# Four rotary-table instructions moved within the value stage, and the doubled keys of mixer B made by GpSimd: a two-layer encoder on one core

## The chip, the cores and the metric

The kernel runs on one core of a Trainium2 chip. Its engines are TensorE (PE in the profile; its weight loads are PEld), VectorE (DVE), ScalarE (ACT), GpSimd (POOL) and SyncE (SP), each with a queue of its own that it works off in order; they wait for each other through semaphores. The metric is the device time of one execution in microseconds (us). Three executions of the kernel before took 1438.0, 1436.29 and 1437.93 us, the median is 1437.93 us.

## The reference

The input is one sequence of 512 positions with 1024 channels, float32. Two layers follow each other; each is a token mixer and a squared-ReLU MLP, with a residual around each:

```python
def reference(x, ...):
    for i in range(DEPTH):                       # DEPTH = 2
        h = rms_norm(x, norm_mix[i])
        if i % 2 == 0: y = dilated_mixer(h, ...) # mixer A
        else:          y = mla_mixer(h, ...)     # mixer B
        x = x + y
        h = rms_norm(x, norm_ffn[i])
        a = jax.nn.relu(h @ w1); x = x + (a * a) @ w2
```

Mixer A projects to queries, keys and values for three groups of eight heads of 128 channels. Queries and keys are normalised per head, scaled by a gain and rotated:

```python
qkv = (h @ w_qkv).reshape(B, S, 3, N_GROUPS, A_HEADS, A_HEAD_DIM)
for g, (window, dil) in enumerate(DIL_CONFIGS):
    q = rope(rms_norm(qkv[:, :, 0, g], q_gain[g]), S)
    k = rope(rms_norm(qkv[:, :, 1, g], k_gain[g]), S)
    o, lse = dilated_group(q, k, qkv[:, :, 2, g], window, dil)
```

`rope(x)` is `x * cos + rot * sin`, where `rot` is x with its halves exchanged and one of them negated. Mixer B is latent attention with eight heads. A key there has 128 channels of its own head and 64 rotated channels that all heads share; the norm runs over all 192:

```python
k = jnp.concatenate([k_nope, broadcast(k_rope)], -1)
k = rms_norm(k, k_gain)
k = jnp.concatenate([k[..., :128], rope(k[..., 128:], S)], -1)
```

## The kernel before, in words

The program is one function, written with a tile framework. Which instruction stands where in an engine's queue is set by the framework's scheduler, by its own forecast of costs, and not only by the order of the code: an edit at one place can move instructions at others. `tc.issue_after(mark)` makes it put what stands under it behind the marked instruction. Pools hand out tiles in turn; a transfer into a tile waits for the last reader of what was there.

All matrix products run in float32 split in two: a weight `b` becomes `whi` (a ScalarE copy, L406 or L157) and `wlo` (VectorE's `b - whi`, L407 or L158), and each product is three matmuls, high by high, high by low, low by high.

**The value stage** (`v_phase`, some 9 to 130 us) makes mixer A's values for six heads of each of the three groups g = 0, 1, 2. Tokens, input channels and output columns are each cut in two, and seven products of blocks replace eight. Group 0 runs first, woven with the norm and the transposition of the input (`norm`, `turn`, `Ssp`, `hT`); `piece(g, ba)` makes products 5, 3, 6, 7 and 4 of a group. Four weight blocks `b11`, `b21`, `b12`, `b22` come by DMA for each group (L328, SP's queue); `add_block` (L334, VectorE, two instructions of 128x768) makes their sums `bT` and `b3`. A product accumulates into two PSUM tiles, and `put` (L433 to L443) brings them to `vo`: a ScalarE copy (L438) for the first, a VectorE add or subtract of 128x384 (L440) for the others. A product that takes the same PSUM tile must wait for that `put`.

After `piece(0, ba)` a tile `rot` gets cosines, sines and gains by three DMAs on SP (L515 and L305), and `tables(0, ...)` (L256 to L265, called at L518) makes group 0's tables from it: four VectorE multiplies of 128x512, `cosg` (L260) and `sing` (L263), two each. Their first reader is the evacuation of queries and keys (`qk_evac`), in the stage after the values. Then the loop over g = 1, 2 does the same seven products with loads one group ahead.

**Mixer B** (some 885 to 1075 us) goes by pairs of heads. For each pair and each 128 positions, `kv_chunk` projects keys and values (matmuls at L1028), sums squares on ScalarE into `junkb` (L137), gets the reciprocal root `krs` (VectorE L129, then a power on GpSimd, L132), and makes `ks`, the scaled keys (VectorE, L1082), and `kd`: the shared rotated key `krr` times the head's `krs`, written twice side by side (ScalarE, L1085, two instructions of 128x128 with `krs` as scale). TensorE transposes `ks` and `kd` (L124), and ScalarE and VectorE bring them out as `kn` (L1095) and `kr` (L1098). `q_chunk` does the like for queries: `r` (VectorE, L1049), `rd` (GpSimd, L1053, 128x256), `qn`, `qr`. `score` and `pv_b` are the attention of the pair (L1110, L1134). There are 16 key chunks in all, four for each of four pairs.

Of the kernel before, what the change touches and what calls it, by code (L numbers as in the profile page):

```python
# [12 lines left out]
AF = mybir.ActivationFunctionType  # L13
ALU = mybir.AluOpType
# [3 lines left out]
P = 128  # L18
# [8 lines left out]
QL, KVL, RD = 256, 128, 64  # L27
# [60 lines left out]
def encoder_kernel(ctx: ExitStack, tc: tile.TileContext, x, norm_mix, norm_ffn, a_w_qkv, a_q_gain, a_k_gain,  # L88
# [3 lines left out]
    V, A, G, PE = nc.vector, nc.scalar, nc.gpsimd, nc.tensor  # L92
    uid = [0]
    marks = {}

    def nm(s):
        uid[0] += 1
        return f"{s}_{uid[0]}"
# [24 lines left out]
    def transpose(o, i):  # L123
        PE.transpose(o, i, ident)  # L124
# [10 lines left out]
    def mean_square(junk, x, dim, out):  # L135

        A.activation(junk, x, AF.Square, scale=1.0 / math.sqrt(dim), accum_out=out)  # L137
# [118 lines left out]
    def tables(g, gqk, cos, sin):  # L256

        for t in range(2):
            gb = gqk[:, t].rearrange("p (f d) -> p f d", f=2).unsqueeze(1).broadcast_to([P, NT, 2, 64])
            V.tensor_tensor(cosg[g][:, :, t].rearrange("p r (f d) -> p r f d", f=2),  # L260
                            cos.rearrange("p (r d) -> p r d", r=NT).unsqueeze(2).broadcast_to([P, NT, 2, 64]), gb,
                            op=ALU.mult)
            V.tensor_tensor(sing[g][:, :, t].rearrange("p r (f d) -> p r f d", f=2),  # L263
                            sin.rearrange("p (r f d) -> p r f d", r=NT, f=2), gb, op=ALU.mult)
# [38 lines left out]
    def load_gains(g, gqk):  # L303
        for t, src in enumerate((a_q_gain, a_k_gain)):
            nc.sync.dma_start(gqk[:, t], src[0, g].partition_broadcast(P))  # L305

    def v_phase(vp):
# [17 lines left out]
        def block(g, ki, ni, name):  # L325
            t = vp.tile([P, 4, VH], F32, tag="wq", name=nm(name), bufs=6)
            for u in range(2):
                nc.sync.dma_start(t[:, 2 * u:2 * u + 2], wblk(g, ki, ni, u))  # L328
            return t

        def add_block(t, x, y):
            for u in range(2):
                us = slice(2 * u, 2 * u + 2)
                V.tensor_tensor(t[:, us], x[:, us], y[:, us], op=ALU.add)  # L334
# [89 lines left out]
        def both(p, w, banks, first):  # L424
            for u, t in ((0, 0), (0, 1), (1, 0), (1, 1)):
                product(p, w, banks, first, u, t)

        def new_banks(chain):
            pl, tg = {"a": (sc_p, "sc"), "b": (tp_p, "tp"), "d": (acc_p, "acc")}[chain]
            return [pl.tile([P, 512], F32, tag=tg, name=nm(tg)) for _ in range(2)]  # L430

        def put(g, i, n, how, banks, last):

            o = vo[:, 2 * i + n]
            for t in range(2):
                acc = banks[t][:, :VH]
                if how == "set":
                    A.activation(o[:, t], acc, AF.Copy)  # L438
                else:
                    V.tensor_tensor(o[:, t], o[:, t], acc, op=ALU.add if how == "add" else ALU.subtract)  # L440
                if last:

                    nc.gpsimd.dma_start(vall[g].rearrange("(m r) d -> m r d", r=NT)  # L443
                                        [:, 2 * i + t, VH * n:VH * n + VH], o[:, t])
# [19 lines left out]
        def sum_tile():  # L464
            return vp.tile([P, 4, VH], F32, tag="wq", name=nm("bT"), bufs=6)
# [48 lines left out]
        rot = vp.tile([P, D], F32, tag="xn", name="rot", bufs=2)  # L514
        nc.sync.dma_start(rot[:, 0:C_M1 - C_KEEP], consts[:, C_KEEP:C_M1])  # L515
        g0 = rot[:, 768:1024].rearrange("p (t d) -> p t d", t=2)
        load_gains(0, g0)
        tables(0, g0, rot[:, 0:256], rot[:, 256:768])  # L518
        for g in range(1, NG):
            b21[g] = block(g, 1, 0, "b21")  # L520
            b11[g] = block(g, 0, 0, "b11")
            b12[g] = block(g, 0, 1, "b12")
            b22[g] = block(g, 1, 1, "b22")
            bT[g] = sum_tile()
            parts = {}
            bd, ba = new_banks("d"), new_banks("a")
            both(2, b21[g], bd, True)
            put(g, 0, 0, "set", bd, False)
            both(1, b11[g], ba, True)
            put(g, 0, 0, "add", ba, True)  # L530
            add_block(bT[g], b11[g], b12[g])
            piece(g, ba)

# [3 lines left out]
    with tc.tile_pool(name="vph", bufs=1, reuse_waits="tile") as vp:  # L537
        v_phase(vp)
# [408 lines left out]
    if True:  # L947
        with tc.tile_pool(name="bpool", bufs=1, reuse_waits="tile") as bp, \
# [22 lines left out]
            krr = bp.tile([P, NT, RD], F32, name="krr")  # L971
# [100 lines left out]
            def kv_chunk(d, r):  # L1072
                acc = proj(d, "wkv", r, 2, 512)
                a4 = acc.rearrange("p (h c d) -> p h c d", h=2, c=2)
                junk = bw.tile([P, QL], F32, tag="junkb", name=nm("junkb"), bufs=1)
                ss = st.tile([P, 8], F32, tag="kss", name=nm("kss"))
                for h in range(2):
                    mean_square(junk[:, 0:DH], a4[:, h, 0], QKD, ss[:, h:h + 1])
                rs = rstd_of(ss[:, 0:2], 2, ssr[:, r:r + 1], "krs")
                A.activation(d["v"][:, r], a4[:, :, 1], AF.Copy)  # L1080
                ks = bw.tile([P, 2, DH], F32, tag="ks", name=nm("ks"), bufs=2)
                V.tensor_tensor(ks, a4[:, :, 0], rs.unsqueeze(2).broadcast_to([P, 2, DH]), op=ALU.mult)  # L1082
                kd = bw.tile([P, 2, 2, RD], F32, tag="kd", name=nm("kd"), bufs=2)
                for h in range(2):
                    A.activation(kd[:, h], krr[:, r].unsqueeze(1).broadcast_to([P, 2, RD]), AF.Copy, scale=rs[:, h:h + 1])  # L1085

                def part2():
                    tp = tp_p.tile([P, 512], F32, tag="tp", name=nm("tp"))
                    for h in range(2):
                        transpose(tp[:, h * P:(h + 1) * P], ks[:, h])  # L1090
                        transpose(tp[:, (2 + h) * P:(3 + h) * P], kd[:, h].rearrange("p c d -> p (c d)"))
                    tv = tp.rearrange("p (c t) -> p c t", c=4)
                    sl = slice(r * P, (r + 1) * P)
                    kn, kr = d["kn"], d["kr"]
                    A.activation(kn[:, :, 0, sl], tv[:, 0:2], AF.Copy, scale=gn[:, 1:2])  # L1095
                    V.scalar_tensor_tensor(kn[:, :, 1, sl], tv[:, 0:2], gn[:, 1:2], kn[:, :, 0, sl].bitcast(F32),
                                           op0=ALU.mult, op1=ALU.subtract)
                    A.activation(kr[:, :, 0, sl], tv[:, 2:4], AF.Copy)  # L1098
                    V.tensor_tensor(kr[:, :, 1, sl], tv[:, 2:4], kr[:, :, 0, sl].bitcast(F32), op=ALU.subtract)
                return part2  # L1100
# [122 lines left out]
```

## Time and profile before

| what | value |
|---|---|
| median of three runs | 1437.93 us |
| the profiled execution, its span | 1438.19 us, 1436.4 us |
| mean clock granted to TensorE | 0.996 |
| PE, DVE, ACT, POOL busy | 1400.1, 938.3, 748.6, 208.4 us |
| chain of work that ended last | PE 88%, DVE 5%, ACT 3%, DMA 2% |

The span runs from the first instruction to the last; the rest of an execution's time lies around it. "PE sc L421 <- DVE vo L440: 4.6, 3, 3.1" reads: TensorE's matmuls of line 421 into tile `sc` waited for the VectorE instruction of line 440 that writes `vo`, 4.6 us in total, three times, at most 3.1 us. In a timeline a row has its start, its duration, engine, line, operation, tiles and shape; "x6" joins six alike, and brackets hold the idle time ahead of it and what ended that. Instructions of VectorE and matmuls overlap at their ends, so the distance from one start to the next is what one costs.

### The profile page before, as it was taken

To read this page: it belongs to the slowest core of one execution; us is meant where nothing else is said; L and a number is where in the kernel's file an instruction comes from. 1 tells how busy PE (TensorE), PEld (TensorE's weight loads), DVE (VectorE), ACT (ScalarE), POOL (GpSimd) and SP (SyncE) were. 2 spreads that over 40 slices of the span, in tenths; PEclk is the share of its full clock that TensorE was granted. 3 is DMA by queue.
4 is the path that set the end of the run, shared out by engine and by line. 5 is a ranking of instruction groups with operands and counts; after the bars stand their busy time and mean duration, and the time that the engine had idled before them with its cause. 6 is when DMAs were issued, how large, how long until landed. Compare 5 with 4: busy or idle time off the path is not lost.

```text
span 1436.4 us, 19249 instructions
## 1 busy us (share of the span) xinstructions
PE 1400.1 (97%) x7044; PEld 1186.7 (83%) x7044; DVE 938.3 (65%) x1497; ACT 748.6 (52%) x1626; POOL 208.4 (15%) x224
## 2 busy tenths in 40 slices
PE   7899999999999999999999999999999999999998
PEld 7899888888888988888888887766768888888886
DVE  6876778676876754465564759688755266475647
ACT  6453656464564623553545455777633453544543
POOL 1111212121112001020110203322201010020201
PEclk9999999999999999999999999999999999999999
DMA  9434322332312345667493854210114759394835
GB/s 321 155 132 143 107 88 66 112 98 79 118 60 78 119 135 183 183 130 222 114 235 101 205 121 92 72 31 30 32 44 161 190 114 238 90 231 134 190 89 117
DMA packets 121086, 185.25 MB, mean 129 GB/s; under 512 B 8416, under 2 KB 58336, under 8 KB 120992
## 3 DMA queue, kind: packets, MB, share of 16 engines
q1 hardware_dynamic: 101808, 144.96, 31.5%
q0 software_dynamic: 19184, 39.07, 15.1%
q8 instruction: 55, 0.90, 0.2%
q14 instruction: 39, 0.32, 0.1%
HBM read 176.13 MB, written 7.86 MB: 128 GB/s over the span
## 4 chain that ended last, share of the span: by engine, by line
PE 88%; DVE 5%; ACT 3%; DMA 2%; issue 1%; SPq 0%; POOL 0%; DVEq 0%; ACTq 0%
PE acc L185 51%; PE sc L848 11%; PE tp L848 7%; PE tp L124 4%; PE sc L421 3%; PE tp L421 2%; PE acc L1134 2%; PE sc L1028 1%; PE acc L1110 1%; DVE wlo L792 1%; PE sco L697 1%; PE sc L583 1%; PE sco L693 1%; DMA b<-in_a_w_qkv_dram 1%; PE sc L1110 1%
## 5 line engine op out<-in xcount | busy, mean ns | idle before, releaser
L185 PE MATMUL acc<-whi,hT 128*128 128x512 f32 (+2 forms) x1216 | 384.3, 390 | 2.6 <-ACT hT L735 1.3
L185 PE MATMUL acc<-hT_f,whi 128*128 128x512 f32 (+1 forms) x1152 | 320.2, 368 | 1.7 <-DVE resid L911 1.2
L158 DVE TENSOR_TENSOR wlo<-raw,whi 128x1024 fp32r<-128x1024 f32 (+3 forms) x146 | 172.1, 1187 | 178.4 <-ACT whi L157 178.1
L185 PEld LDWEIGHTS acc<-whi,hT 128*128 128x128 f32 x1216 | 225.3, 188 | 42.7 <-ACT hT L735 1.9
L185 PEld LDWEIGHTS acc<-hT_f,whi 128*128 128x128 f32 x1152 | 209.3, 190 | 37.3 <-DVE resid L911 1.6
L185 PE MATMUL acc<-wlo,hT 128*128 128x512 f32 (+2 forms) x608 | 235.9, 389 | 0.0
L157 ACT ACTIVATE whi<-raw 128x1024 fp32r<-128x1024 f32 (+3 forms) x146 | 149.8, 1031 | 162.0 <-PE acc L185 67.9
L792 DVE TENSOR_TENSOR wlo<-wqs,whi 128x1024 fp32r<-128x1024 f32 x112 | 137.8, 1231 | 112.6 <-ACT whi L791 112.5
L185 PE MATMUL acc<-hT_f,wlo 128*128 128x512 f32 (+1 forms) x576 | 205.6, 367 | 0.0
L791 ACT ACTIVATE whi<-wqs 128x1024 fp32r<-128x1024 f32 x112 | 118.8, 1061 | 159.8 <-PE acc L185 65.8
L848 PE MATMUL sc<-whi,asp 128*128 128x512 f32 x512 | 165.0, 390 | 0.8 <-DVE resid L822 0.7
L777 POOL DMA_DIRECT2D wqs<-in_ffn_w_dram x64 | 77.6, 1344 | 547.9 <-DVE wlo L792 365.0
L185 PEld LDWEIGHTS acc<-wlo,hT 128*128 128x128 f32 x608 | 114.4, 188 | 18.7 <-issue 0.2
L185 PEld LDWEIGHTS acc<-hT_f,wlo 128*128 128x128 f32 x576 | 109.2, 190 | 17.6
L848 PE MATMUL tp<-whi,asp 128*128 128x512 f32 x352 | 112.2, 390 | 1.8 <-DVE resid L822 1.8
L848 PEld LDWEIGHTS sc<-whi,asp 128*128 128x128 f32 x512 | 96.1, 188 | 21.5 <-issue 1.6
L132 POOL TENSOR_TENSOR qrs<-rs_v,nhalf 128x4 f32<-128x4 f32 x48 | 58.7, 1228 | 288.8 <-DVE rs_v L129 239.7
L848 PE MATMUL sc<-wlo,asp 128*128 128x512 f32 x256 | 99.6, 389 | 0.0
L137 ACT ACTIVATE junk<-acc 128x128 f32<-128x128 f32 x192 | 53.1, 277 | 55.7 <-PE acc L185 50.6
L848 PEld LDWEIGHTS tp<-whi,asp 128*128 128x128 f32 x352 | 66.1, 188 | 16.4 <-DVE resid L822 2.7
L848 PE MATMUL tp<-wlo,asp 128*128 128x512 f32 x176 | 68.2, 389 | 0.0
L295 ACT ACTIVATE qkT<-tp 128x512 f32<-128x512 f32 x48 | 35.8, 765 | 51.2 <-PE tp L124 50.9
(231 smaller groups left out, 2194.2 us busy)
## 6 DMA issues: line engine op xcount, KB each, us to landing
wqs<-in_ffn_w_dram SPq DMA_DIRECT2D x80, 512.0 KB, 5.2
raw<-in_ffn_w_dram SPq DMA_DIRECT2D x64, 512.0 KB, 4.4
wqs<-in_ffn_w_dram POOLq DMA_DIRECT2D x64, 512.0 KB, 7.1
raw<-in_a_w_qkv_dram SPq DMA_DIRECT2D x96, 256.0 KB, 3.1
b<-in_a_w_qkv_dram SPq DMA_DIRECT2D x24, 384.0 KB, 5.8
vall<-vo POOLq DMA_DIRECT2D x24, 192.0 KB, 2.4
raw<-in_a_w_o_dram SPq DMA_DIRECT2D x8, 512.0 KB, 3.8
raw<-in_b_w_o_dram SPq DMA_DIRECT2D x8, 512.0 KB, 3.7
```

The costliest lines, as they stand in the source:

```text
L124: PE.transpose(o, i, ident)
L132: G.tensor_tensor(out, v[:, :n], nhalf[:, :n], op=ALU.pow)
L137: A.activation(junk, x, AF.Square, scale=1.0 / math.sqrt(dim), accum_out=out)
L157: A.activation(hi[:, :nk, :n], raw[:, :nk, :n], AF.Copy)
L158: V.tensor_tensor(lo[:, :nk, :n], raw[:, :nk, :n], hi[:, :nk, :n].bitcast(F32), op=ALU.subtract)
L185: PE.matmul(accs[o][:, oc], lhsT=lt, rhs=rt, start=(kt == 0 and p_i == 0 and hv == 0), stop=(kt == total - 1 and p_i == 2), skip_group_che ...
L295: A.activation(dst, tv, AF.Copy)
L421: PE.matmul(banks[t][:, :VH], lhsT=lt, rhs=rt[:, j], start=(first and k == 0 and i_ == 0), stop=(k == 3 and i_ == 2), skip_group_check=True)
L777: marks["sum"] = nc.gpsimd.dma_start(t, src, accum_op=ALU.add).ins
L791: A.activation(hi, x, AF.Copy)
L792: V.tensor_tensor(lo, x, hi.bitcast(F32), op=ALU.subtract)
L848: PE.matmul(bk[t], lhsT=lt, rhs=rt[:, j], start=(first and k == 0 and i_ == 0), stop=(k == 3 and i_ == 2), skip_group_check=True)
```

## The change

The call of `tables(0, ...)` goes from the end of group 0 into the loop, at g = 1 behind the second `put`, and is issued behind that `put`'s last instruction. `kd` is made by one GpSimd multiply of 128x256 in place of two ScalarE instructions of 128x128. Lines behind L440 are one further down in the changed kernel, those behind the loop four.

```diff
                 else:
-                    V.tensor_tensor(o[:, t], o[:, t], acc, op=ALU.add if how == "add" else ALU.subtract)
+                    marks["put"] = V.tensor_tensor(o[:, t], o[:, t], acc,
+                                                   op=ALU.add if how == "add" else ALU.subtract).ins
...
         load_gains(0, g0)
-        tables(0, g0, rot[:, 0:256], rot[:, 256:768])
         for g in range(1, NG):
...
             put(g, 0, 0, "add", ba, True)
+            if g == 1:
+
+                with tc.issue_after(marks["put"]):
+                    tables(0, g0, rot[:, 0:256], rot[:, 256:768])
             add_block(bT[g], b11[g], b12[g])
...
                 kd = bw.tile([P, 2, 2, RD], F32, tag="kd", name=nm("kd"), bufs=2)
-                for h in range(2):
-                    A.activation(kd[:, h], krr[:, r].unsqueeze(1).broadcast_to([P, 2, RD]), AF.Copy, scale=rs[:, h:h + 1])
+                G.tensor_tensor(kd, krr[:, r].unsqueeze(1).unsqueeze(1).broadcast_to([P, 2, 2, RD]),
+                                rs.unsqueeze(2).unsqueeze(2).broadcast_to([P, 2, 2, RD]), op=ALU.mult)
```

In VectorE's queue, where the tables stood, in the middle of group 0; `wlo_396` is the low part of a weight, `dif`, `Ssp` and `hT` come from the transposed input. First the rows before, then those of the change:

```order
L387 TENSOR_TENSOR Ssp_113<-dif,Ssp_113 128x4x128
L260 TENSOR_TENSOR cosg_103<-rot 128x4x128
L158 TENSOR_TENSOR wlo_396<-raw_149,whi_395 128x2x384
L390 TENSOR_TENSOR dif<-dif,h_111 128x512
L263 TENSOR_TENSOR sing_104<-rot 128x4x128
L260 TENSOR_TENSOR cosg_103<-rot 128x4x128
L263 TENSOR_TENSOR sing_104<-rot 128x4x128
L387 TENSOR_TENSOR Ssp_115<-dif,Ssp_115 128x4x128
L374 TENSOR_TENSOR hT_91<-tp_300,hT_91 128x4x128
```

```order
L387 TENSOR_TENSOR Ssp_113<-dif,Ssp_113 128x4x128
L158 TENSOR_TENSOR wlo_396<-raw_149,whi_395 128x2x384
L390 TENSOR_TENSOR dif<-dif,h_111 128x512
L387 TENSOR_TENSOR Ssp_115<-dif,Ssp_115 128x4x128
L374 TENSOR_TENSOR hT_91<-tp_300,hT_91 128x4x128
```

The four rows of `cosg` and `sing` are gone; they stand behind the second `vo` of group 1 now, directly ahead of a `wlo` of product 6.

Further down the same queue, around the first `vo` adds of group 0; `b_70_542` is group 0's `b3`, `bT_675` (`bT_671` in the change) group 1's sum of `b11` and `b12`, `b_84` and `b_85` those two blocks. Before, and then the change:

```order
L334 TENSOR_TENSOR b_70_542<-b_9_143,b_10_146 128x768 x2
L440 TENSOR_TENSOR vo<-vo,sc_154 128x384
L387 TENSOR_TENSOR Ssp_116<-dif,Ssp_116 128x4x128
L407 TENSOR_TENSOR wlo_584<-b_70_542,whi_583 128x2x384
L334 TENSOR_TENSOR bT_675<-b_84_666,b_85_669 128x768
L407 TENSOR_TENSOR wlo_600<-b_70_542,whi_599 128x2x384
L334 TENSOR_TENSOR bT_675<-b_84_666,b_85_669 128x768
L407 TENSOR_TENSOR wlo_620<-bT_384,whi_619 128x2x384
L334 TENSOR_TENSOR b_110_824<-b_85_669,b_86_672 128x768 x2
L440 TENSOR_TENSOR vo<-vo,sc_155 128x384
```

```order
L334 TENSOR_TENSOR b_70_542<-b_9_143,b_10_146 128x768 x2
L407 TENSOR_TENSOR wlo_546<-bT_384,whi_545 128x2x384
L387 TENSOR_TENSOR Ssp_116<-dif,Ssp_116 128x4x128
L407 TENSOR_TENSOR wlo_562<-bT_384,whi_561 128x2x384
L334 TENSOR_TENSOR bT_384<-bT_384,b_4_122 128x768 x2
L407 TENSOR_TENSOR wlo_584<-b_70_542,whi_583 128x2x384
L334 TENSOR_TENSOR bT_671<-b_84_662,b_85_665 128x768 x2
L407 TENSOR_TENSOR wlo_600<-b_70_542,whi_599 128x2x384
L440 TENSOR_TENSOR vo<-vo,sc_154 128x384
L407 TENSOR_TENSOR wlo_620<-bT_384,whi_619 128x2x384
L440 TENSOR_TENSOR vo<-vo,sc_155 128x384
```

The first `vo` now comes behind both `wlo` of `b3`, behind `Ssp_116` and behind group 1's `bT`; the second comes ahead of `b_110`, behind which it stood. The load of `b_85` (SP) waits for the second `b_70_542` row in place of the second `bT_384` row behind it.

GpSimd's queue in the first pair of mixer B in the changed kernel; `kd_1348` belongs to the second key chunk, `kd_1356` to the third:

```order
L993 TENSOR_TENSOR krr_7804<-krr_7804,kr2_1327_8015 128x64
L132 TENSOR_TENSOR krs_1346_8065<-rs_v_1345_8063,nhalf_86 128x2
L132 TENSOR_TENSOR krs_1354_8091<-rs_v_1353_8089,nhalf_86 128x2
L1088 TENSOR_TENSOR kd_1348_8070<-krr_7804,krs_1346_8065 128x256
L1088 TENSOR_TENSOR kd_1356_8096<-krr_7804,krs_1354_8091 128x256
L132 TENSOR_TENSOR rqs0_75<-rs_v_1360_8109,nhalf_86 128x2
L1057 TENSOR_TENSOR rd_1364_8119<-rt_1362_8114,r2_1363_8115 128x256
L132 TENSOR_TENSOR krs_1370_8140<-rs_v_1369_8138,nhalf_86 128x2
L132 TENSOR_TENSOR rqs0_75<-rs_v_1384_8200,nhalf_86 128x2
L1088 TENSOR_TENSOR kd_1372_8145<-krr_7804,krs_1370_8140 128x256
```

Before, these rows stood there without the `kd`; the second chunk's `kd` now follows the third chunk's `krs`. The queue has 16 rows more, and ScalarE's has 32 fewer.

## The prediction

> **What bounds the kernel now.** I read the engines' busy row first, then TensorE's waits, then the two places where these waits stand.
>
> ```profile
> span 1436.4 us, 19249 instructions
> PE 1400.1 (97%) x7044; PEld 1186.7 (83%) x7044; DVE 938.3 (65%) x1497; ACT 748.6 (52%) x1626; POOL 208.4 (15%) x224
> ...
> PE tp L124 <- DVE xn L361: 9.0, 1, 9.0
> PE sc L421 <- DVE vo L440: 4.6, 3, 3.1
> ...
> PE sc L1028 <- ACT junkb L137: 2.0, 1, 2.0
> ```
>
> TensorE (PE) is busy for 97%, and neither edit gives it or takes from it a matmul. Time can be won only from its waits, and from the stretches in which its clock is halved. The largest wait, 9.0 us at the start, is not touched. The second, on `vo` (the add that frees a pair of accumulators), lies in the stage that makes mixer A's values, behind the place of the tables. The last one shown lies at the start of mixer B, where ScalarE makes the doubled keys `kd`.
>
> For the first place the timelines of VectorE and of TensorE (start, duration, instruction; in brackets the idle time ahead and its releaser):
>
> ```profile
> 31.74 0.69 DVE L260 TENSOR_TENSOR cosg<-rot 128x512 f32<-128x512 f32 x1 [1.17 <-DMA rot<-in_a_q_gain_dram]
> 32.35 0.95 DVE L158 TENSOR_TENSOR wlo<-raw,whi 128x768 fp32r<-128x768 f32 x1
> 33.22 0.68 DVE L390 TENSOR_TENSOR dif<-dif,h 128x512 f32<-128x512 f32 x1
> ...
> 61.43 0.55 DVE L440 TENSOR_TENSOR vo<-vo,sc 128x384 f32<-128x384 f32 x1
> ...
> 38.16 0.61 PE L185 MATMUL acc<-whi,hT 128*128 128x384 f32 x2 [0.40 <-DVE hT L374]
> ...
> 54.55 0.41 PE L421 MATMUL sc<-whi,Ssp 128*128 128x384 f32 x1 [1.39 <-DVE vo L440]
> ...
> 62.03 0.44 PE L421 MATMUL sc<-whi,Ssp 128*128 128x384 f32 x1 [3.05 <-DVE vo L440]
> ```
>
> VectorE waits 1.17 us for `rot`, and from there to 61.4 it has hardly a gap: it is the bound of group 0, and TensorE waits three times for it. By the pitch of the starts a 128x768 instruction costs 0.87 us (32.35 to 33.22) and, over the four of the tables, 0.60 us for 128x512. Next, in windows of 1 us (columns: busy time and count of PE, PEld, DVE, ACT, POOL; granted clock; DMA share; GB/s), and one of the whole piece:
>
> ```profile
> 63.00:64.00 1.00, 1.00 (x5) 1.00 (x5) 0.31 (x1) 0.61 (x1) 0.40 (x1) 0.65 0.79 187
> 64.00:65.00 1.00, 1.00 (x4) 1.00 (x4) 0.73 (x1) 0.24 (x1) 0.15 (x1) 0.50 0.97 330
> 65.00:66.00 1.00, 1.00 (x5) 1.00 (x5) 0.78 (x2) 0.74 (x1) 0.00 (x0) 0.50 1.08 401
> 66.00:67.00 1.00, 1.00 (x5) 1.00 (x4) 0.86 (x1) 0.10 (x1) 0.54 (x1) 0.64 0.97 341
> ...
> 38.15:68.05 29.90, 25.34 (x131) 24.34 (x132) 27.38 (x36) 14.81 (x23) 4.40 (x7) 0.94 0.47 145
> ...
> 53.06:56.47 3.41, 1.92 (x10) 1.59 (x10) 3.41 (x6) 2.09 (x3) 0.56 (x1) 1.00 0.87 264
> ...
> 920.05:923.46 3.41, 1.40 (x10) 1.28 (x9) 2.23 (x9) 3.38 (x18) 1.93 (x4) 1.00 0.15 60
> ```
>
> After the 3.05 us wait the clock is short by 0.35 + 0.50 + 0.50 + 0.36 = 1.71 us: a wait here costs more than itself. The last two rows are 3.41 us, twice 1.71, long. In the first TensorE idles 1.5 us and full clock follows; in the second it idles 2.0 us and half clock follows (shown below). So some 1.5 to 2 us of idling within such a window decides.
>
> [...]
>
> **The change part by part: tables.** Four instructions of 0.60 us leave the head of VectorE's queue in group 0. VectorE no longer waits for `rot`, but its next instruction needs ScalarE:
>
> ```profile
> 30.51 0.85 ACT L157 ACTIVATE whi<-raw 128x768 fp32r<-128x768 f32 x1 [0.67 <-DMA raw<-in_a_w_qkv_dram]
> ...
> 74.30 4.16 PE sc L421 x24
> ```
>
> `whi` ends at 31.36, so `wlo` starts at about 31.42 in place of 32.35: 0.9 us, not 1.17. Behind it three more tables are gone, 1.8 us, so VectorE runs 2.7 us early. TensorE's 0.40 us wait at 38.16 goes and it starts there at about 37.6: **0.55 us** (an estimate by what VectorE has ahead of it).
>
> The new order, however, puts other work ahead of the first `vo` add. From that `wlo` there are 17 instructions of 128x768 and 15 of 128x512 now: 17 x 0.87 + 15 x 0.60 = 23.8 us, so the add starts at 31.42 + 23.8 = 55.2, and TensorE's matmul behind it at about 55.95, where before it was 54.55. TensorE has more to do ahead of it, the rest of the `tp` products: it comes there at about 54.3 and waits some 1.65 us. The second add follows at about 56.8, one 128x768 instruction behind it, before its reader comes up: the 3.05 us wait has gone.
>
> Undisturbed, a matmul of this stage takes 4.16/24 = 0.173 us, and 132 of them 22.9 us. They took 29.9 us: 7.0 us over, made of 4.44 us of waits, 1.71 us of half clock and the rest for restarting. After the change I put 1.65 us plus 0.3 us for one restart there: 7.0 - 1.95 = 5.05 us, with the 0.55 **5.6 us** won in group 0. If the new wait halves the clock itself, it is 1.7 us less.
>
> One transfer hangs on this. A sum of the second group's weights (`bT<-b,b`) now also stands ahead of the first add, and its load is released by another instruction:
>
> ```profile
> 52.23 11.58 SPq L328 DMA_DIRECT2D b<-in_a_w_qkv_dram  x8
> ...
> 55.80 0.95 DVE L334 TENSOR_TENSOR bT<-b,b 128x768 f32<-128x768 f32 x1
> ...
> DMA to landing us min/median/max: 3.4/5.8/7.9
> ```
>
> Before, the load was issued at 52.23 and used at 55.80 without waiting, so it took at most 3.6 us. Now it is issued behind the second `b3` add, at about 47.9, and needed at 55.2 - 3 x 0.87 = 52.6: 4.7 us. I take no wait, since SP's row, the only one from 40 to 66 us, leaves nothing issued shortly before it; the median landing would make 1.1 us, the longest 3.2 us.
>
> The new place, behind the second add of group 1 (VectorE's rows with their idle time):
>
> ```profile
> 81.50 0.96 DVE L407 TENSOR_TENSOR wlo<-bT,whi 128x768 fp32r<-128x768 f32 x1 [1.16 <-ACT whi L406]
> ...
> 83.91 0.96 DVE L407 TENSOR_TENSOR wlo<-bT,whi 128x768 fp32r<-128x768 f32 x1 [0.46 <-ACT whi L406]
> ...
> 88.56 0.96 DVE L407 TENSOR_TENSOR wlo<-b,whi 128x768 fp32r<-128x768 f32 x1 [0.83 <-ACT whi L406]
> 89.93 0.56 DVE L440 TENSOR_TENSOR vo<-vo,sc 128x384 f32<-128x384 f32 x1 [0.42 <-PE sc L421]
> ...
> 95.81 0.44 PE L421 MATMUL sc<-whi,hT 128*128 128x384 f32 x1 [0.19 <-DVE vo L440]
> ...
> 129.98 5.03 PE acc L185 x22
> ```
>
> Here VectorE has 1.16 + 0.46 + 0.83 + 0.42 = 2.9 us of idle time to hide 4 x 0.60 = 2.4 us. Not every gap lies where the tables delay something, and the wait at 95.81 should grow from 0.19 to some 0.65: **0.45 us lost**; between nothing and 2.4 us if nothing were hidden. The tables' first reader comes with the queries' projection behind 129.98, 48 us later. Stage in all: 5.6 - 0.45 = **5.2 us**.
>
> **Keys.** ScalarE gives up 32 instructions, GpSimd (POOL) takes 16 of twice the size. The rows of both, the two stretches, and the crowded start of mixer B:
>
> ```profile
> L1085 ACT ACTIVATE kd<-krr,krs x32: 388/411/517, 917.0 to 1016.2; 128x128 f32<-128x128 f32 x32
> L1053 POOL TENSOR_TENSOR rd<-rt,r 128x256 f32<-128x256 f32 x16 | 11.8, 739 | 9.1 <-DVE r L1049 8.0 <-ACT junkb L137 0.6
> 917.00:931.00 14.00, 10.64 (x50) 7.73 (x49) 9.42 (x39) 13.37 (x58) 8.29 (x13) 0.88 0.22 70
> ...
> 918.75 0.72 ACT L1085 ACTIVATE kd<-krr,krs 128x128 f32<-128x128 f32 x2
> 919.33 0.50 ACT L1095 ACTIVATE kn<-tp,gn 128x256 fp32r<-128x256 f32 x1
> ...
> 919.43 0.70 POOL L132 TENSOR_TENSOR krs<-rs_v,nhalf 128x2 f32<-128x2 f32 x1 [1.14 <-DVE rs_v L129]
> ...
> 922.18 1.29 PE L1028 MATMUL sc<-w,cT 128*128 128x384 f32 x6 [2.01 <-ACT junkb L137]
> ...
> 924.00:925.00 1.00, 1.00 (x6) 0.82 (x5) 0.78 (x4) 0.97 (x6) 0.84 (x2) 0.50 0.00 0
> ```
>
> ScalarE is busy 13.37 of 14 us here: it is the bound, and TensorE waits 2.01 us for it and then runs at half clock. A pair of `kd` costs ScalarE 0.58 us (918.75 to 919.33). Three pairs stand ahead of the `junkb` for which TensorE waits: 1.74 us. For GpSimd the nearest row is `rd`, same engine, stage and shape: 0.74 us, 11.8 us in all, of which 5 fall in these 14 us: 3.7 us, where GpSimd has 14 - 8.29 = 5.7 us free. `rd` too reads its operands repeated; that `kd` repeats one value over all columns may cost something. The upper bound stands at (c) below.
>
> One `kd` comes later than before: on GpSimd the second chunk's stands behind the third chunk's `krs` (919.43), at 919.9 to 920 in place of 919.47. Even so TensorE's matmuls of 922.18 start at about 920.9, 1.3 us early; the half clock behind (1.7 us) should fall out, and two shorter waits of together 0.9 us that are new come in behind the late transposes: 1.3 + 1.7 - 0.9 = **2.1 us**. In the later pairs `kd` stands in few steps of the chain, and the order of the other instructions changes too: +0.2 us, taken between -1 and +1. Sum for mixer B **2.3 us**, between -1 us, if the new waits halve the clock as the old one did and the reorder loses, and +4 us.
>
> [...]
>
> **Sum.** 5.2 + 2.3 = 7.5 us. The profiled execution took 1438.2 us (its span 1436.4, 1.8 lie around it), 0.3 us over the median of 1437.93: 1438.2 - 7.5 = 1430.7 us.
>
> **The rivals.** (a) Only part of it comes: the new 1.65 us wait lies between the 1.5 us that kept the clock and the 2.0 us that halved it, so it may halve it (1.7 us), or mixer B's new waits do: 1438.2 - 7.5 + 1.7 to 3.4 = 1432.4 to 1434.1. For it: such a window is cut where it falls. Against it: it needs most of the wait inside one window.
>
> (b) The load is late in group 0: at 7.9 us the add is 3.2 us late and the half clock is back, 7.5 - 3.2 - 1.7 = 2.6 us left, 1435.6 us; with half of mixer B's gain missing too, 1436.7. Against it speak the idle queue and the 3.6 us of before.
>
> (c) The other side: GpSimd becomes the bound of mixer B. Its instructions stretch where VectorE reads two operands at the same time:
>
> ```profile
> 873.46 1.44 POOL L966 TENSOR_TENSOR cgB<-ck,gr 128x128 f32<-128x128 f32 x1
> ...
> 876.26 0.45 POOL L966 TENSOR_TENSOR cgB<-ck,gr 128x128 f32<-128x128 f32 x1
> ```
>
> The same instruction took 1.44 us and 0.45 us, 3.2 times. At that rate a `kd` takes 2.4 us, five 12 us, 6.3 us over the 5.7 free; with one more half clock (1.7) and the 5.2 won before: 1438.2 - 5.2 + 6.3 + 1.7 = 1441.0. It decides from (5.7 + 5.2)/5 = 2.2 us a `kd` on. Against it: `rd` in the same stage averages 0.74 us.
>
> [...]
>
> (d) More: mixer B's later pairs gain as well, 1427 to 1428.
>
> **How the numbers follow.** Forecast 0.55, (a) 0.19, (b) 0.12, (c) 0.08, (d) 0.06. A run tells 0.2% from no change, 2.9 us: below 1435.1 is faster, above 1440.8 slower. Faster: forecast, (a), (d) less some spill, 0.77; same: (b) and spill, 0.15; slower: (c), 0.08. The range of 1427 to 1437 leaves out (c) and the ends of (b) and (d).
>
> **What would show it.** Right: no idle time of VectorE ahead of `wlo` at 31.4; one wait on `vo` of 1 to 2 us near 55 and none of 3 us; full clock from 62 to 68; the piece that ended at 68.05 done near 62.6; the first pair in mixer B with no wait over 1 us and no half clock; `kd` at 0.7 to 0.8 us on POOL. Wrong: a DMA as releaser of VectorE between 50 and 56, half clock behind 56, tables that push a wait at 95 beyond 1 us, `kd` over 1.1 us, or TensorE waiting for `kd` in several pairs.

## The result

The changed kernel takes 1428.78 us (median of 4 executions, 1427.53 to 1429.46), beside 1437.97 us before (1436.29 to 1438.85): ratio 0.9937, 95% interval 0.9919 to 0.9954, some 9.2 us. Forecast were 1430.7 us and a range of 1427 to 1437. The profiled execution of after took 1427.53 us.

The page and the waits of TensorE after the change:

```profile
span 1425.8 us, 19234 instructions
PE 1394.0 (98%) x7044; PEld 1183.8 (83%) x7044; DVE 939.6 (66%) x1497; ACT 740.5 (52%) x1594; POOL 217.2 (15%) x240
...
PE sc L1032 <- DVE ks L1086: 2.4, 2, 1.2
PE sc L421 <- DVE vo L440: 2.0, 2, 1.4
```

The same 7044 matmuls are busy for 6 us less: part of the gain is clock, and it isn't seen among the waits. Where the time went is read from three rows of each kernel. Each row stands for the instructions of one line, with their count, their durations (least, median, most) and their first and last start. Read from them are the last start of the value stage's matmuls, the first of mixer B's projections, and the first score of mixer B's last pair. Before, and then after:

```profile
L421 PE MATMUL sc<-whi,hT x96: 334/334/522, 15.7 to 129.6; 128*128 128x384 f32 x96
...
L1028 PE MATMUL acc<-w,cT x12: 390/400/504, 912.2 to 919.6; 128*128 128x512 f32 x12
...
L1110 PE MATMUL sc<-kn,qn x24: 389/389/478, 1030.7 to 1060.2; 128*128 128x512 f32 x24
```

```profile
L421 PE MATMUL sc<-whi,hT x96: 334/334/522, 15.5 to 124.8; 128*128 128x384 f32 x96
...
L1032 PE MATMUL acc<-w,cT x12: 390/398/504, 907.3 to 914.2; 128*128 128x512 f32 x12
...
L1114 PE MATMUL sc<-kn,qn x24: 389/389/478, 1021.6 to 1051.0; 128*128 128x512 f32 x24
```

| stretch | before | after | won |
|---|---|---|---|
| to the end of the value stage | 129.6 | 124.8 | 4.8 us |
| from there to mixer B's first projection | 782.6 | 782.5 | 0.1 us |
| mixer B, from its first projection to the last pair's scores | 118.5 | 114.3 | 4.2 us |
| from there to the end of the span | 405.7 | 404.2 | 1.5 us |

The last line of the table is not the change's: at the start of the second MLP both kernels have the same waits, and before the clock was halved behind them while it was not in this execution of after. It is taken up under the last experiment. Without it the table adds up to 9.1 us, the gain of the medians.

### The profile page after: what moved, and what is told of

Read it like the earlier page. It is cut to its first block, busy times and chain, and to the rows that moved or that the text cites. A ratio compares the mean times of both kernels' runs of the same rounds, so it can differ in the third digit from the quotient of the medians.

```text
span 1425.8 us, 19234 instructions
## 1 busy us (share of the span) xinstructions
PE 1394.0 (98%) x7044; PEld 1183.8 (83%) x7044; DVE 939.6 (66%) x1497; ACT 740.5 (52%) x1594; POOL 217.2 (15%) x240
## 4 chain that ended last, share of the span: by engine, by line
PE 89%; DVE 6%; ACT 2%; issue 1%; DMA 1%; POOL 0%; SPq 0%; DVEq 0%; ACTq 0%; POOLq 0%
PE acc L185 51%; PE sc L852 11%; PE tp L852 7%; PE tp L124 4%; PE sc L421 3%; PE acc L1138 1%; PE sc L1032 1%; PE acc L1114 1%; PE tp L421 1%; DVE wlo L796 1%; PE sco L701 1%; PE sc L587 1%; PE acc L421 1%; PE sco L697 1%; DVE wlo L407 1%
```

## The profile after, at the two places

The value stage on VectorE and on TensorE (start, duration, instruction; in brackets the idle time ahead and its releaser):

```profile
31.36 0.96 DVE L158 TENSOR_TENSOR wlo<-raw,whi 128x768 fp32r<-128x768 f32 x1 [1.04 <-ACT whi L157]
...
55.69 0.54 DVE L440 TENSOR_TENSOR vo<-vo,sc 128x384 f32<-128x384 f32 x1
...
57.02 0.54 DVE L440 TENSOR_TENSOR vo<-vo,sc 128x384 f32<-128x384 f32 x1
...
56.38 0.41 PE L421 MATMUL sc<-whi,Ssp 128*128 128x384 f32 x1 [1.40 <-DVE vo L440]
...
86.54 0.41 PE L421 MATMUL sc<-whi,Ssp 128*128 128x384 f32 x1 [0.62 <-DVE vo L440]
```

The first add is at 55.69 (forecast 55.2), the second at 57.02 (56.8), and in group 0 TensorE waits 1.40 us once (1.65) and not a second time. No DMA holds up VectorE's sums there. In group 1 a wait of 0.62 us stands at 86.54. It is not the one that was forecast at 0.65 us: that one, 95.81 in the kernel before, belongs to the third of four adds and is gone, and the new one belongs to the first of them.

Mixer B as a whole, before:

```profile
912.20:1030.70 118.50, 109.87 (x544) 82.26 (x545) 96.74 (x292) 94.72 (x333) 35.78 (x51) 0.99 0.14 43
```

Mixer B after, as a whole, then GpSimd's keys, the window that the prediction took (the work stands 4.9 us further on in it now), and TensorE's waits there:

```profile
907.30:1021.60 114.30, 106.88 (x545) 81.41 (x545) 98.30 (x292) 86.63 (x301) 44.52 (x67) 1.00 0.14 45
...
L1088 POOL TENSOR_TENSOR kd<-krr,krs 128x256 f32<-128x256 f32 x16 | 9.8, 616 | 1.0
...
917.00:931.00 14.00, 12.41 (x68) 9.52 (x66) 11.10 (x36) 11.14 (x44) 8.10 (x13) 1.00 0.00 0
...
916.20 1.29 PE L1032 MATMUL sc<-w,cT 128*128 128x384 f32 x6 [0.59 <-DVE rs_v L129]
...
918.81 1.29 PE L1032 MATMUL sc<-w,cT 128*128 128x384 f32 x6 [0.88 <-DVE r L1053]
...
921.69 0.47 PE L1032 MATMUL sc<-whi,cT 128*128 128x512 f32 x1 [0.65 <-DVE rs_v L129]
```

A `kd` takes 0.616 us (forecast 0.74, from `rd`). The one wait of 2.01 us has become waits under 1 us here, which VectorE's reciprocal roots (`rs_v`) and rotations (`r`) end, and the clock is 1.00 where it was 0.88.

The larger part of the gain lies further on. Measured from mixer B's first projection, the first score of the second pair comes after 44.1 us before and 42.3 after, that of the third pair after 79.2 and 75.1. Between the two, TensorE's long waits before were for ScalarE's copies `pTs`; after, they are gone and one for `ks` remains. Before, and then after:

```profile
965.74 3.70 PE L1134 MATMUL acc<-pTs,vb 128*128 128x512 f32 x8 [0.63 <-ACT pTs L1126]
...
980.60 3.70 PE L1134 MATMUL acc<-pTs,vb 128*128 128x512 f32 x8 [1.48 <-ACT pTs L1126]
```

```profile
970.69 0.41 PE L1032 MATMUL sc<-whi,cT 128*128 128x384 f32 x1 [1.20 <-DVE ks L1086]
```

## The experiments

My theory was that the two edits add up, and that in the value stage the tables' 2.4 us on VectorE and the wait for their tile had been the cause. The rivals: the gain is the new order that the scheduler made of it, or it is a matter of where the clock's windows fall. Where a run has the clock halved in a stage, that is said with it.

### Each edit alone

Tables moved, `kd` as before:

```diff
-                G.tensor_tensor(kd, krr..., rs..., op=ALU.mult)
+                for h in range(2):
+                    A.activation(kd[:, h], krr..., AF.Copy, scale=rs[:, h:h + 1])
```

> The move of the tables alone, the keys left on ScalarE. My theory (the two edits add up, each in its own stage): the value stage ends as in the changed kernel, its last matmul at about 124.8 us in place of 129.6, 4.8 us early, and mixer B keeps its 118.5 us, with the 2.0 us wait and a half clock behind it; 1438.0 - 4.8 = 1433.2 us. Rival (mixer B's gain is a matter of where the clock's window falls): mixer B, started 4.8 us earlier, loses its half clock without any edit of its own and takes 116.8 us; 1431.5 us.

1432.98 us, ratio 0.9969 (0.9958 to 0.9979). In the profiled execution the value stage ends at 124.5 us, and mixer B takes 117.8 us, without a half clock though the wait of 2.0 us for `junkb` is there. This execution also lost 1.4 us between the two stages: near 815 us ScalarE waited 3.0 us for the DMA of a weight (`wqs`), and TensorE then 0.9 us for a `whi`. Neither edit touches that.

Keys on GpSimd, tables at their old place (the reverse diff):

> The keys alone on GpSimd, the tables at their old place. My theory: the value stage as before, last matmul at 129.6 us with waits of 1.4 and 3.1 us, and mixer B 4.2 us shorter (114.3 in place of 118.5); 1438.0 - 4.2 = 1433.8 us. Rival (window of the clock): mixer B gains only the 1.2 us of idle time, or nothing; 1436 to 1438 us.

1431.93 us, ratio 0.9961 (0.9946 to 0.9975). Mixer B takes 114.1 us. In the value stage this execution has a wait of 2.76 us where before had 3.05, and no half clock behind it:

```profile
61.75 0.44 PE L421 MATMUL sc<-whi,Ssp 128*128 128x384 f32 x1 [2.76 <-DVE vo L440]
...
L421 PE MATMUL sc<-whi,hT x96: 333/334/525, 15.9 to 127.8; 128*128 128x384 f32 x96
...
57.23:60.64 3.41, 1.77 (x11) 1.45 (x9) 3.37 (x5) 1.12 (x2) 0.00 (x0) 1.00 0.54 196
```

Each edit works in its own stage, as forecast: the stage that a run leaves alone has the old order of instructions in these traces. But both stages' figures of before hold a half clock that isn't always there. Without it the value stage of the old order ends at 127.8 us, so the move wins 3.0 to 3.3 us and the half clock is the other 1.5 to 1.8. Mixer B with the keys on ScalarE takes 117.8 us without it and 118.5 with it, in the same order but for one `kn`, so the keys win 3.5 to 3.7 us and the half clock was worth 0.7 there: TensorE idles 9.1 us in the first and 8.6 in the second, so part of what it lost it would have waited. The rival on the clock's window is right on these parts, and wrong on the rest. It also helps explain why the two gains, 4.7 and 5.7 us in the medians, add up to more than 9.2: in their profiled executions each of the single runs also lacks the half clock of the other stage.

### What in the value stage the move of the tables won

The load put back: four VectorE multiplies behind the first `Ssp` (the mark `ssp`), where the tables had stood, on the norm's gains.

```diff
         load_gains(0, g0)
+        with tc.issue_after(marks["ssp"]):
+            for t in range(2):
+                for x in (cosg[0], sing[0]):
+                    V.tensor_tensor(x[:, :, t], gain_b[:, 0:512]..., gain_b[:, 512:1024]..., op=ALU.mult)
```

> The changed kernel with four more VectorE multiplies of 128x512 at the tables' old place, on data that is there long before, their output overwritten by the tables later (wasted work): the 2.4 us of load are back, the wait for the late tile is not. Three theories. The load: it costs what the move won, value stage ending at 128 to 129.6 us as before. The wait for the tile: nearly all of the gain stays, 125 us. The order: the second of group 0's adds stands ahead of the sums that wait for a load, as in the changed kernel, so the 3.05 us wait and its half clock stay away although the load is back; the first wait is near 1 us; end at 125 to 126 us, 1429 to 1430 us.

1429.23 us, ratio 0.9941 (0.9924 to 0.9957).

```profile
32.96 0.69 DVE L522 TENSOR_TENSOR sing<-g_mix 128x512 f32<-128x512 f32 x1
...
53.26 0.55 DVE L440 TENSOR_TENSOR vo<-vo,sc 128x384 f32<-128x384 f32 x1
...
57.20 0.55 DVE L440 TENSOR_TENSOR vo<-vo,sc 128x384 f32<-128x384 f32 x1
...
57.80 0.45 PE L421 MATMUL sc<-whi,Ssp 128*128 128x384 f32 x1 [0.89 <-DVE vo L440]
...
L421 PE MATMUL sc<-whi,hT x96: 334/334/443, 15.3 to 124.7; 128*128 128x384 f32 x96
```

The four instructions are back on VectorE ahead of both adds, and the stage ends at 124.7 us as without them, so their load does not by itself cost the 3 us. It is no clean test of what the load does cost, because the scheduler made a third order of it: the first add stands ahead of both `wlo` of `b3` and of group 1's `bT` here and comes at 53.26 us, 2.4 us earlier than in the changed kernel. The tile's wait is gone in this run, so it remains, beside the order. Two runs put the tables back as they were, with their wait, and only hold sums of weight blocks back, behind the fourth add of the group before. In both, VectorE's other instructions of this stage stand in the order of the kernel before, so they are the clean test. The mark `hold` is the last add of product 7 of group g - 1. The first run holds `b3` alone:

```diff
-            add_block(b3, b12[g], b22[g])
+            if g:
+                with tc.issue_after(marks["hold"]):
+                    add_block(b3, b12[g], b22[g])
+            else:
+                add_block(b3, b12[g], b22[g])
...
+            marks["hold"] = marks["put"]
...
+        tables(0, g0, rot[:, 0:256], rot[:, 256:768])
```

> The tables at their old place on VectorE, the keys on GpSimd as changed, and only the second sums of groups 1 and 2 (the ones called b3, which wait for the last load of a group) held behind the fourth add of the group before. If the order around the second add was the cause of the 3.05 us wait, that wait falls to 0.3 us or less with the tables still in front: the value stage ends at about 125 us, against 129.6 us before and 127.8 us in the run of the keys alone, where the clock was not halved in this stage; 1429 us. If the tables' 2.4 us and the wait for their tile were the cause, it ends at 127.8 us or later, 1432 us.

1429.55 us, ratio 0.9934 (0.9916 to 0.9953).

```profile
38.60 0.62 PE L185 MATMUL acc<-whi,hT 128*128 128x384 f32 x2 [1.15 <-DVE hT L374]
...
60.31 0.44 PE L421 MATMUL sc<-whi,Ssp 128*128 128x384 f32 x1 [0.88 <-DVE vo L440]
...
L421 PE MATMUL sc<-whi,hT x96: 334/334/522, 15.1 to 125.7; 128*128 128x384 f32 x96
```

The wait is 0.88 us, not 0.3, and the stage ends at 125.7, not 125: the size is off, the direction clear. In the run of the keys alone, with the same tables and the sums in the old order, it was 2.76 us and 127.8. Part of what is missing is `rot`: VectorE waited 2.34 us for it here and 1.14 there, and its tables started 0.4 us later. The second run holds `bT` of groups 1 and 2 in the same way:

> As the run with only the second sums held, and the first sums (bT) held there as well; the tables at their old place. By the order theory the wait ahead of the first add stays at 1.4 us, since VectorE's queue up to that add is that of the kernel before, and all later waits on these adds go: end at 124.0 to 124.8 us, that is 1.4 to 2 us behind the version with the tables moved too (122.7 us). By the tables theory it ends at 127 us or later.

1427.43 us, ratio 0.992 (0.990 to 0.994).

```profile
54.28 0.41 PE L421 MATMUL sc<-whi,Ssp 128*128 128x384 f32 x1 [1.41 <-DVE vo L440]
...
L421 PE MATMUL sc<-whi,hT x96: 334/334/343, 15.7 to 123.8; 128*128 128x384 f32 x96
```

With the tables at their old place, load and wait included (0.71 us for `rot` here), the stage ends 1.0 us earlier than in the changed kernel. So the order of the sums and the adds is enough for the whole gain. In the changed kernel the scheduler had put `b3` behind the second add once the tables were gone; by the run with `b3` alone that place is worth 2.1 us of the 3.0 to 3.3, and some 2.5 (an estimate) if the later `rot` is allowed for. How the rest divides between load, wait and `bT` isn't shown.

### Both: a faster version

The changed kernel with the tables moved and all these sums held:

> The changed kernel, with the sums of weight blocks for groups 1 and 2 held behind the fourth add of the group before, where VectorE idles 3.1 and 2.9 us. If VectorE's queue ahead of the adds is what TensorE waits for, the waits of 1.40 and 0.62 us go, with their restarts some 2.2 us: value stage ending at about 122.6 in place of 124.8, 1426.6 us. Rival (the loads of the next blocks, which wait for these sums, come late, or the wait only moves to a later add): no gain or a loss, 1428.8 us or more.

1427.15 us, ratio 0.9926 (0.9911 to 0.9941). The stage ends at 122.7 us: VectorE makes the sums where it idled 3.09 us in the changed kernel (ahead of 66.03 us, for ScalarE's `whi`), and the 1.40 us wait is gone. Beside the changed kernel on one chip:

> The changed kernel once more, beside the version with the sums held on the same chip: 1428.8 us; the value stage ends at 124.8 us, mixer B takes 114.3 us.

> The version with all sums of groups 1 and 2 held, beside the changed kernel on the same chip: 2.1 us less than it by the end of the value stage (122.7 against 124.8 us), 1426.7 us, with single executions of both apart by 1.7 us according to whether a half clock falls at the start of the second MLP.

The changed kernel took 1428.51 us (1428.03 to 1428.70), this version 1426.83 us (1425.77 to 1428.02). Its value stage (that of the changed kernel ends at 124.6 us in this run):

```profile
L421 PE MATMUL sc<-whi,hT x96: 334/334/343, 15.0 to 122.6; 128*128 128x384 f32 x96
```

TensorE waits 0.67 and 0.45 us there, once for a `wlo` and once for an add of group 1. Against the run with the tables in front (123.8, a single execution), the move itself is worth 1.1 to 1.2 us once the sums are held.

### The tables on GpSimd

For group 0, E is GpSimd here, and the call stands at its old place:

```diff
-            V.tensor_tensor(cosg[g]..., op=ALU.mult)
+            E.tensor_tensor(cosg[g]..., op=ALU.mult)
```

> The changed kernel with the tables made by GpSimd at their old place. If GpSimd and VectorE slow each other where VectorE reads two operands from SBUF, as the rows of 1.44 and 0.45 us suggested, the four take some 4 us each in place of 1.3, VectorE's instructions beside them stretch by about a fifth, some 3 us in all, and the value stage ends at 126.5 to 128 us in place of 124.8. If they don't, VectorE is freed of another 2.4 us in group 1 and the wait of 0.62 us goes: 124.2 us.

1430.71 us, ratio 0.9951 (0.9936 to 0.9966), the stage ends at 127.1 us. GpSimd, then VectorE:

```profile
31.47 1.68 POOL L260 TENSOR_TENSOR cosg<-rot 128x512 f32<-128x512 f32 x1 [4.43 <-DMA rot<-in_a_q_gain_dram]
...
33.11 1.74 POOL L263 TENSOR_TENSOR sing<-rot 128x512 f32<-128x512 f32 x1
34.81 1.74 POOL L260 TENSOR_TENSOR cosg<-rot 128x512 f32<-128x512 f32 x1
...
31.93 1.77 DVE L390 TENSOR_TENSOR dif<-dif,h 128x512 f32<-128x512 f32 x1
33.62 1.78 DVE L387 TENSOR_TENSOR Ssp<-dif,Ssp 128x512 fp32r<-128x512 f32 x1
35.32 0.68 DVE L374 TENSOR_TENSOR hT<-tp,hT 128x512 fp32r<-128x512 f32 x1
```

The two get in each other's way, as expected, by 2.3 us at the end of the stage; VectorE's order is that of the changed kernel but for a few instructions of group 1. The sizes are other than expected: GpSimd's four take 1.7 us each, not 4, and two of VectorE's instructions with both operands in SBUF (`dif` and `Ssp`) go from 0.68 to 1.77 us, while `hT`, which reads one from PSUM (`tp`), keeps its 0.68 us beside the third table (34.81). What holds them up isn't shown; what the rows show is fixed distances between the ends. VectorE's two end at 33.70 and 35.40 us, each 0.55 us after the multiply that GpSimd had begun before them (33.15, 34.85). GpSimd's next two end at 34.85 and 36.55 us, each 1.15 us after the VectorE instruction that was running when they started. The two rows of 1.44 and 0.45 us in the kernel before go with this: the first (873.46) ran beside VectorE's `wlo<-wqs,whi` (873.09 to 875.98), both operands in SBUF, the second (876.26) beside `resid<-resid,tp` and `resid<-resid,sc` (875.90 and 876.50, 0.67 us each), one operand of each in PSUM.

### What in mixer B the keys won

ScalarE's load put back, GpSimd still makes the keys:

```diff
                 G.tensor_tensor(kd, krr..., rs..., op=ALU.mult)
+                for h in range(2):
+                    A.activation(spare[:, h], krr..., AF.Copy, scale=rs[:, h:h + 1])
```

> The changed kernel, with ScalarE still doing its 32 instructions of 128x128 in mixer B, into a tile that nobody reads (wasted work; the keys come from GpSimd). If the load taken off ScalarE is what shortens mixer B, the 0.58 us a chunk come back: mixer B at 117 to 118.5 us and 1431.5 to 1433 us. If the gain is the new order, or the place of the half clock, mixer B stays near 114.3 and the time near 1429 us.

1431.51 us, ratio 0.9956 (0.9941 to 0.9971). Mixer B takes 117.2 us, with no half clock in it. The stretch of 912 to 926 us in the run of the tables alone, in the changed kernel, and in this one:

```profile
912.00:926.00 14.00, 10.17 (x54) 7.03 (x52) 9.88 (x40) 13.71 (x63) 9.15 (x14) 1.00 0.25 75
```

```profile
912.00:926.00 14.00, 10.85 (x60) 8.09 (x60) 11.47 (x42) 11.81 (x51) 11.37 (x19) 1.00 0.22 72
```

```profile
912.00:926.00 14.00, 10.48 (x58) 7.72 (x58) 11.29 (x41) 13.17 (x58) 10.54 (x18) 1.00 0.22 72
```

(Mixer B starts 1.2 us later in the first of them.) ScalarE, the fourth pair of numbers, is busy 13.7, 11.8 and 13.2 us of 14. Of the 3.5 us between the first and the second, 2.9 come back with the load. The load doesn't come back alone, though: the scheduler also changed the order of ScalarE's, VectorE's and TensorE's queues, so this run by itself doesn't tell load from order. What speaks for the load is the chain of work that ended last. Before, it runs without a break over ScalarE from 917.3 to 922.1 us, up to the wait of 2.01 us, and `kd` is in it:

```profile
918.89 0.58 ACT kd L1085 x2
...
920.60 0.58 ACT kd L1085 x2
```

Over the whole of mixer B, `kd` on ScalarE is 2.9% of that chain before and 3.4% in the run of the tables alone, 3.4 and 4.0 us, beside the 3.5 that were won; here the wasted copies are 2.4 us of it. TensorE's waits for `pTs`, which the second pair had before, are back too: 0.77 us at 959.33 and 1.10 at 974.77.

Keys on VectorE:

```diff
-                G.tensor_tensor(kd, krr..., rs..., op=ALU.mult)
+                V.tensor_tensor(kd, krr..., rs..., op=ALU.mult)
```

> The changed kernel with the keys made by VectorE. [...] My theory: VectorE is busy for 11.1 of 14 us at the start of mixer B and its adds and scalings are what TensorE waits for there, 16 x 0.3 us more on it cost part of that: mixer B at 115 to 116.5 us, 1430 to 1431 us.

1429.35 us, ratio 0.9939 (0.9924 to 0.9954).

```profile
L1088 DVE TENSOR_TENSOR kd<-krr,krs x16: 415/418/550, 912.5 to 1008.4; 128x256 f32<-128x256 f32 x16
```

Mixer B takes 115.8 us, but with a half clock of 1.71 us at 916; without it, 114.1 if all of that was lost. An execution without any half clock says the same: one of this run and one of the changed kernel have a mean clock of 1.000, with spans of 1425.9 and 1425.8 us. So my expectation falls: VectorE had the room as well, at 0.42 us an instruction (the 0.3 was my estimate) and in yet another order of the queues. Which of the two engines takes the keys off ScalarE makes no difference that these runs can tell.

Keys made twice on GpSimd (the multiply written two times):

> The changed kernel with each key multiply on GpSimd done twice (wasted work): 16 x 0.61 us more. If GpSimd has room, as its 8.1 of 14 us at the start say, mixer B gets 0.5 to 1 us longer and the time is 1429.3 to 1430 us. If GpSimd is near its limit in the first pair, the transposes of the keys come late: 3 us or more, 1432 us.

1433.45 us, ratio 0.9964 (0.9951 to 0.9977). Mixer B takes 118.9 us, at least 117.2 without the half clock of 1.70 us at 915: 2.9 us or more above the run with one, where I had expected 0.5 to 1.

```profile
PE sc L1032 <- DVE r L1053: 3.9, 3, 2.2
...
914.00:920.00 6.00, 4.05 (x17) 3.32 (x17) 4.00 (x15) 4.32 (x21) 6.00 (x10) 0.72 0.17 56
```

So the idle share of a 14 us window did not tell what fits: GpSimd (the fifth pair of numbers) is busy without a gap from 914 to 920 us here. What carries the loss to TensorE stays open. TensorE waits 3.9 us for VectorE's rotations `r`, where the changed kernel has 1.4, but the chain of work that ended last has no GpSimd row in mixer B here; it reaches those rotations over ScalarE's `kn`, `qs` and `qn`. And the order of the queues is another one in this run too.

### The second MLP's start

The third half clock of before (1.71 us, from 1100.9 on) stands behind waits that no run of this study changes, the longest 1.35 or 1.36 us in each. In the changed kernel's first profiled execution, and then in its repetition, the wait, the 3.41 us around it and the 3.41 us behind:

```profile
1091.08 0.66 PE L124 MATMUL tp<-ck,xn 128*128 128x128 f32 x4 [1.35 <-DVE hT_f L229]
...
1089.12:1092.53 3.41, 1.83 (x14) 1.64 (x15) 2.75 (x6) 1.75 (x3) 0.55 (x1) 1.00 1.01 357
1092.53:1095.94 3.41, 3.41 (x31) 3.41 (x30) 2.44 (x3) 1.54 (x2) 0.00 (x0) 1.00 1.05 371
```

```profile
1090.69 0.66 PE L124 MATMUL tp<-ck,xn 128*128 128x128 f32 x4 [1.35 <-DVE hT_f L229]
...
1088.62:1092.03 3.41, 1.72 (x13) 1.53 (x14) 2.75 (x6) 1.75 (x3) 0.55 (x1) 1.00 1.01 354
1092.03:1095.44 3.41, 3.41 (x19) 3.41 (x18) 2.50 (x3) 1.06 (x1) 0.00 (x0) 0.50 1.01 361
```

The same kernel, the same wait, once full clock and once half. Of the 14 profiled executions of this study 9 have it here, 5 have not; the last stretch of the table takes some 1.5 us more with it.

The clock records of the traces show what differs. Each of the 13 half clocks between 20 and 1415 us lasts 3.41 us and starts a whole multiple of 3.413 us after the clock first rises to full, which is at 17.32 us in the first of these executions and at 16.83 in the second; the three of before start at 63.30, 923.46 and 1100.95 us, 252 and 52 such steps apart. So by these traces the windows lie on a fixed grid of 3.413 us, at another place in each execution, and a wait is cut where a border falls. What the half clocks go by there is how long TensorE is busy within one window. Of the 14 traces' windows between 20 and 1415 us, all ten with TensorE busy for 1.75 us or less were followed by half clock, none with 2.05 or more; in between there are both. Of the waits above, the 2.01 us of before lay wholly inside one window (920.05 to 923.46, 1.40 us busy). The 2.76 us in the run of the keys alone were cut at 60.64, and the 2.0 us in the run of the tables alone at 917.07.

## Why the prediction was right, and where it was not

- **The sum:** 7.5 us forecast, 9.2 us measured: the sign was right and the time, 1428.8, lies between the likeliest case (1430.7) and case (d) (1427 to 1428). Two errors of the sum partly cancel: the value stage won 0.4 us less than forecast, mixer B 1.9 us more.
- **The value stage's size was nearly right, its cause was not.** Forecast 5.2 us, measured 4.8. The single steps came within 0.5 us: `wlo` at 31.36, the adds at 55.69 and 57.02, the wait of 1.40. At the end of the piece 4.7 us were won instead of 5.6, and behind it nothing was lost where 0.45 had been put, so there is some luck in the total; the wait of 0.62 us in group 1 fits the forecast 0.65 in size only. The sign "no idle time of VectorE ahead of `wlo`" did not come, 1.04 us stand there for ScalarE's `whi`, as the sum itself had reckoned. But the step "Four instructions of 0.60 us leave the head of VectorE's queue ... so VectorE runs 2.7 us early" was written as a main part of what wins. With tables and wait both back and the sums held, the stage ends at 123.8 us, earlier than with the tables gone; load and wait are worth 1.1 to 1.2 us beside that. What decides is the sentence further down: that the second add stands one 128x768 instruction behind the first, and no longer behind `b3`, two instructions and a wait for a load. The forecast counted the new order correctly and took it for a side effect, where it alone is enough.
- **Half clocks: the term was treated as certain, and in mixer B it was too large.** 1.71 us in the value stage and 1.7 us in mixer B were taken as won for good. The old order does without them at times: 2.76 us of waiting without one in the run of the keys alone, the 2.0 us wait in the run of the tables alone. Not often, though: in 20 of the 26 executions of the kernel before that stand beside the experiments the mean clock is 0.996 or 0.995, what three half clocks make. In mixer B the half clock was worth 0.7 us, not 1.7. The reading that some 1.5 to 2 us of idling within a window decide comes near what the grid shows (1.4 to 1.7); what it lacked is that the windows don't follow the waits.
- **Mixer B was mis-sized, and in the wrong place.** 2.3 us forecast, 4.2 measured, just beyond the upper bound of 4. The step that failed is "In the later pairs ... +0.2 us": up to the second pair's first score 1.8 us are won, beside the 2.1 forecast for the first pair, and behind it 2.4 us, nearly all in the second pair, where ScalarE's late `pTs` had held up TensorE for 0.63 and 1.48 us. Without half clocks 3.5 us are won, where the forecast has 1.3 - 0.9 + 0.2 = 0.6. ScalarE's load as the cause fits all runs (2.9 us of it come back, and the chain shows `kd` with 3.4 to 4.0 us); that the new order has no part in it isn't shown, since with each change of this load the order changed too. By the rows of the whole stage without half clocks, TensorE's idle time falls by 1.7 us (117.8 - 108.7 = 9.1 to 114.3 - 106.9 = 7.4) and its busy time by 1.8; where the busy time comes from wasn't tried.
- **GpSimd's price:** 0.74 us forecast, 0.616 measured; case (c) from 2.2 us a `kd` on didn't come near. But the reason given, 5.7 us free in 14, is weak: by it the doubled keys would have fitted, and they cost 2.9 us.
- **The late load** of case (b) did not show: VectorE's sums stand in the timeline without a DMA as releaser. The load was issued at 48.24 us and used at 53.08 without a wait, so it took at most 4.8 us.
- **Keys on VectorE:** an instruction takes 0.42 us there and 0.62 on GpSimd, 1.5 times as long. For the kernel it makes no difference that these runs can tell: without a half clock the spans are 1425.9 us with the keys on VectorE and 1425.8 on GpSimd.

## What to carry to other kernels

When an edit takes work out of a busy queue under a scheduler, compare the order of what is left first: here holding four sums of weight blocks behind the adds won 4.0 us and moving the tables 3.0 to 3.3 (both beside the 127.8 us without a half clock), and the first could have been had without the second. Check the order of a test kernel as well, since putting a load back can change it too. Look for the releases (adds that free an accumulator) that stand behind instructions which wait for a transfer, and for a gap a few us further on into which those fit. Book a half clock that follows a wait as a chance and not as a sum: the border of a window can cut the wait, as it did at 60.64 us with the 2.76 us of the run of the keys alone, and the same wait of 1.35 us brought a half clock in 9 of 14 executions. Don't take an engine's idle share of a long window for room: GpSimd had 5.7 of 14 us free in the kernel before, and the doubled keys cost 2.9 us.

## What the runs showed of the hardware

- Every one of the 13 half clocks between 20 and 1415 us lasted 3.41 us and took 1.70 to 1.71 us of full clock. They start on a grid of 3.413 us that differs from execution to execution. In the 14 traces all ten windows of that stretch with TensorE busy for at most 1.75 us were followed by one, none with 2.05 us or more. The same wait of 1.35 us (with shorter ones around it) brought one in 9 of 14 executions.
- What a half clock cost the kernel was 1.5 to 1.8 us in the value stage, some 1.5 us at the second MLP and 0.7 us in mixer B.
- A 128x512 VectorE instruction with both operands in SBUF took 1.77 us beside a running GpSimd multiply instead of 0.68 in two instances, and 0.68 in one with an operand from PSUM; GpSimd's own took 1.68 to 1.74 us. The slowed ones ended a fixed time after the other engine's (0.55 us on VectorE, 1.15 us on GpSimd, twice each). In mixer B, where instructions that read PSUM make 77 of VectorE's 114 us (in the changed kernel, the durations from 907 to 1022 us added up), `kd` took 613 to 625 ns in all 16, and few of VectorE's means rose, by at most about 0.05 us (`pe` from 500 to 545 ns, `wlo` of 128x1024 from 1220 to 1272).
